# Six start addresses for the transposed input of a hybrid SSD / DeltaNet trunk

## The chip, the cores and the metric

The kernel runs on one core of one Trainium2 chip. The metric is the device time of one execution in microseconds (us); the time before is the median of three runs.

A core has a matrix engine (PE, or TensorE) that multiplies a stationary operand, loaded into its array beforehand, with a moving operand that streams past it; a vector engine (DVE), a scalar engine (ACT), GpSimd (POOL) and SyncE (SP), whose queue issues the transfers here. Operands lie in an on-chip memory of 128 partitions (SBUF); an address below is the byte offset inside a partition. Matrix products are gathered in another on-chip memory (PSUM).

## What is computed

A trunk of two layers on 256 tokens of width 1024. Each layer has three sub-layers, a feed-forward network (FFN), a token mixer, and a second FFN, and each sub-layer starts from a root-mean-square norm of the residual stream:

```python
h = x
for l in range(DEPTH):                                   # DEPTH = 2
    h = h + 0.5 * swiglu(rms_norm(h, ffn1_norm[l]), ffn1_w_in[l], ffn1_w_out[l])
    u = rms_norm(h, mix_norm[l])
    (z_s, xbc, dt_s, qkv, z_d, b_d, a_d, gate_s, gate_d) = split(u @ w_in[l])
    y_s = mamba2_branch(z_s, xbc, dt_s, ...)
    y_d = deltanet_branch(qkv, z_d, b_d, a_d, ...)
    merged = sigmoid(gate_s) * (y_s @ ssm_w_branch[l]) + sigmoid(gate_d) * (y_d @ dn_w_branch[l])
    h = h + merged @ w_out[l]
    h = h + 0.5 * swiglu(rms_norm(h, ffn2_norm[l]), ffn2_w_in[l], ffn2_w_out[l])
return rms_norm(h, final_norm)
```

## The kernel before

**Numbers in two halves.** Every float32 operand of the large products is split into two float32r numbers: a high half, which is the value rounded by ACT, and a low half, the rest, which DVE subtracts. A product a·b is made as three matmuls, high·high, high·low and low·high (`mm3`, `mm3w`).

**The weights.** They stream from device memory in pieces of 128 x 1024 floats. `load` puts a piece into one of five buffers (`wraw`, or `wfirst`), `prep` splits it into `whi` and `wlo`, each with five buffers of 4096 bytes, and `take` hands a piece to the matmuls while it loads and splits the following ones ahead. So a buffer of `whi` or `wlo` comes free when the matmuls have read it.

**The transposed input.** `norm_in`, once for each sub-layer, normalises the residual stream, transposes it on PE (`hnT`) and lets ACT write the high halves and DVE the low halves into `uT` (`rms_chain`). `uT` is one tile of 16384 bytes per partition: for each of the eight blocks of 128 input channels (`kt`) 256 tokens of high halves and then 256 tokens of low halves. It is written once for each of the six sub-layers, and always at the same place.

**Who reads `uT`.** Two kinds of code, which use it in opposite roles:

- `tok_chunk` gives tokens by output channels. The stationary operand is a 128 x 128 slice of `uT`, the moving operand 512 columns of `whi` or `wlo`; lines 287 to 289 (in `mm3`). It makes the tiles `f` (the first chunk of an FFN, 48 matmuls) and `t` (`z` and gate chunks of the mixer, eight units of 48 matmuls in each mixer, so 384).
- `chan_chunk` and `chan_pair` give output channels by tokens. The stationary operand is a 128 x 128 slice of `whi` or `wlo`, the moving operand is `uT`. `chan_pair` (tile `fc`, 20 groups of 16 pairs, so 320 pairs, in each FFN) makes a matmul of 512 columns, the high and the low half of one `kt` together (line 342), and one of 256 columns (line 346). `chan_chunk` (tiles `kk`, `qq`, `vv`, `zd`, `bc`, `xs` of the mixer) makes three matmuls of 256 columns each (lines 292 to 294).

The other large products don't read `uT`: the output products of the FFN (`p`, `o`), the branch products (`b`) and the output product of the mixer (`o` with `mh` and `ml`) have other stationary tiles and moving weights, through `mm3` as well.

**Where things lie.** `uT` starts at byte 32928, which is 160 modulo 256. All buffers of `whi` and `wlo` start at 128 modulo 256 (78464 is the first), and so do `gh`, `gl`, `bsa`, `bsb`, `bsc`, `bh`, `bl`, `mh` and `ml`, the stationary tiles of the other products. All steps inside these tiles that a matmul starts at are multiples of 512 bytes. So every slice of `uT` starts at 160 modulo 256, and every other operand of the large products at 128: the weights lie 224 bytes behind `uT` modulo 256, or, seen from the weights, `uT` lies 32 bytes behind them.

**Order.** The order of work is the program's own, by `FFN` and `ORDER`; a scheduler moves the steps of the norm ahead (`high_priority`). Each engine runs its own list in order.

Of the kernel before, what the change touches and what calls it, by code (L numbers as in the profile page):

```python
# [8 lines left out]
F32R = mybir.dt.float32r  # L9
# [7 lines left out]
P = 128  # L17
D = 1024
S = 256
# [3 lines left out]
KT = D // P  # L23
# [6 lines left out]
NRAW = 5  # L30
NSPL = 5
START = 2

# [16 lines left out]
def trunk_kernel(ctx, tc, x, wst, wsm, norms, lpar, rpar, cst, out):  # L52
# [3 lines left out]
    cpool = ctx.enter_context(tc.tile_pool(name="cpool", bufs=1))  # L56
# [25 lines left out]
    def tmp2(name):  # L82
        return s2.tile([P, 512], F32, tag="s2", name=name)
# [92 lines left out]
    def ahead(key, n, fn):  # L176
        while state[key] < n:
            fn(state[key])
            state[key] += 1
# [47 lines left out]
    Y = [cpool.tile([P, 512], F32, name=f"Y{i}") for i in range(2)]  # L227
    for y in Y:
        G.memset(y[:], 0.0)
    uT = cpool.tile([P, KT, 2, S], F32R, name="uT")  # L230
    uTh, uTl = uT[:, :, 0], uT[:, :, 1]

    def rstd_of(t):

# [9 lines left out]
    def rms_chain(t, nw):  # L244
        r = rstd_of(t)
        hns = []
        for n in range(2):
            hn = tmp2("hn")
            ins = stt(hn[:], h[:, t, n * 512 : (n + 1) * 512], r, nw[n], ALU.mult, ALU.mult)
            hns.append(hn)  # L250
        for n in range(2):
            bank = trb("hnT")
            for k in range(4):
                PE.transpose(bank[:, k * P : (k + 1) * P], hns[n][:, k * P : (k + 1) * P], ident)
            oh = uTh[:, 4 * n : 4 * n + 4, t * P : (t + 1) * P]
            ol = uTl[:, 4 * n : 4 * n + 4, t * P : (t + 1) * P]
            bv = bank[:].rearrange("p (k t) -> p k t", k=4)
            done = [act(oh, bv), tt(ol, bv, f(oh), ALU.subtract)]
        return ins, done

    def norm_in(nw, add=None):

        for t in range(2):
            with tc.high_priority(offset=PRI), ExitStack() as behind:
                if add:
                    add(t)
                    if t == 0:
                        behind.enter_context(tc.issue_after(state["sums"][5].ins))
                ins, done = rms_chain(t, nw)
            if t == 0:  # L270
                state["hold"] = False
                n = state["taken"]
                if not add:
                    ahead("prepped", n + 1, prep)
                    with tc.issue_after(done[0].ins), tc.issue_after(done[1].ins):
                        ahead("prepped", n + START, prep)
                with tc.issue_after(ins.ins):
                    ahead("prepped", n + 2, prep)
                if add:
                    state["behind"][n + 2] = [d.ins for d in done]  # L280
            elif add:

                state["behind"][n + 4] = (state["square"].ins, ins.ins)
                state["input"] = done
# [88 lines left out]
    def residual(po, nw):  # L373
        def add(t):
            for n in range(2):
                hv = h[:, t, n * 512 : (n + 1) * 512]
                stt(hv, po[t][n][:], 0.5, hv, ALU.mult, ALU.add)

        if nw is None:
            return add  # L380
        norm_in(nw, add)
# [154 lines left out]
    def mixer(l, nxt):  # L536
# [686 lines left out]
        close(po, stat, 8, nxt)  # L1223

    norm_in(nw0)
    for l in range(DEPTH):
        ffn(norm_vec(3 * l + 1))
# [3 lines left out]
    for t in range(2):  # L1231
        add(t)
        o = [tmp2("fo") for _ in range(2)]
# [141 lines left out]
```

## Time and profile before

| what | us |
|---|---|
| median of three runs | 1569.11 |
| lowest and highest run | 1568.77 and 1569.37 |
| span of the profiled execution, first to last instruction | 1565.8 |
| PE busy in that span | 1545.0 |
| DVE busy | 1302.4 |
| ACT busy | 999.8 |

The record of the profiled execution gives its span; it lies 3.3 us below the median of the runs, which also hold what comes before the first and after the last instruction.

The profile names an instruction by its line in the kernel, its engine and `out<-in`, the tile that it writes and the tiles that it reads. A matmul's duration in it is modelled and overlaps with that of the next one, so the pace of PE is read from the starts of instructions that follow one another, not from their durations. The chain of waits is followed back from the last instruction, at each step to whatever released it. The six sub-layers begin, by the start of their first `hnT`, at 7.0, 189.4, 600.2, 783.2, 964.9 and 1375.1 us.

### The profile page before, as it was taken

How to read it: one execution, taken by the hardware profiler on the slowest of the kernel's cores; microseconds unless marked ns; L12 is line 12 of the kernel's file. 1: busy time of each engine (PE TensorE's matmuls, PEld its weight loads, DVE VectorE, ACT ScalarE, POOL GpSimd, SP SyncE). 2: the span in 40 equal slices, each digit the busy share in tenths (PEclk: the TensorE clock that was granted, in tenths of full speed). 3: DMA queues.
4: the chain of work that ended last, by engine and by line, in shares of the span. 5: the costliest groups of instructions: out<-in, count | busy, mean ns of one | idle time of the engine just before them, and what ended most of it. 6: DMA issues, size and time to landing. Idle time of an engine off the chain costs nothing.

```text
span 1565.8 us, 26672 instructions
## 1 busy us (share of the span) xinstructions
PE 1545.0 (99%) x10152; PEld 1342.0 (86%) x10152; DVE 1302.4 (83%) x2048; ACT 999.8 (64%) x1694; POOL 53.2 (3%) x60
## 2 busy tenths in 40 slices
PE   8999999999999999999999999999999999999998
PEld 6888779999888888888788887899998888888886
DVE  6889969957899766899878998699579996679897
ACT  6666668766675655666566676686656666466664
POOL 0000010000000000000000001010000000000000
PEclk9999999999999999999999999999999999999999
DMA  8565565553455555465765566555336546555553
GB/s 298 197 214 188 195 212 173 178 158 118 174 207 173 177 205 196 159 210 177 262 204 187 168 198 223 189 189 189 116 123 213 177 166 212 201 175 166 198 189 134
DMA packets 94215, 292.99 MB, mean 187 GB/s; under 512 B 22325, under 2 KB 23301, under 8 KB 93062
## 3 DMA queue, kind: packets, MB, share of 16 engines
q1 hardware_dynamic: 94086, 291.29, 55.2%
q8 instruction: 79, 1.29, 0.3%
q14 instruction: 50, 0.41, 0.1%
HBM read 289.33 MB, written 1.92 MB: 186 GB/s over the span
## 4 chain that ended last, share of the span: by engine, by line
PE 76%; DVE 13%; DMA 5%; issue 3%; ACT 2%; POOL 1%; SPq 0%; POOLq 0%; DVEq 0%; ACTq 0%
PE fc L342 15%; PE fc L346 8%; DVE wlo L69 7%; PE t L287 3%; PE t L288 3%; PE t L289 3%; DMA wraw<-in_wst_dram 3%; PE b L289 3%; PE b L288 3%; PE b L287 2%; PE xs L292 2%; PE xs L293 2%; PE xs L294 2%; PE o L288 1%; PE o L289 1%
## 5 line engine op out<-in xcount | busy, mean ns | idle before, releaser
L69 DVE TENSOR_TENSOR wlo<-wraw,whi 128x1024 fp32r<-128x1024 f32 x488 | 591.0, 1221 | 139.8 <-ACT whi L66 136.1
L66 ACT ACTIVATE whi<-wraw 128x1024 fp32r<-128x1024 f32 x488 | 511.6, 1057 | 176.4 <-PE b L289 29.8
L342 PE MATMUL fc<-uT,whi 128*128 128x512 f32 x1280 | 445.5, 391 | 0.0
L346 PE MATMUL fc<-uT,wlo 128*128 128x256 f32 x1280 | 360.9, 282 | 0.0
L342 PEld LDWEIGHTS fc<-uT,whi 128*128 128x128 f32 x1280 | 240.3, 188 | 50.7
L346 PEld LDWEIGHTS fc<-uT,wlo 128*128 128x128 f32 x1280 | 241.8, 189 | 0.8
L287 PE MATMUL t<-whi,uT 128*128 128x512 f32 x256 | 102.9, 403 | 0.0
L288 PE MATMUL t<-wlo,uT 128*128 128x512 f32 x256 | 101.5, 396 | 0.2 <-DVE wlo L69 0.2
L289 PE MATMUL t<-whi,uT 128*128 128x512 f32 x256 | 101.5, 397 | 0.0
L66 ACT ACTIVATE whi<-wfirst 128x1024 fp32r<-128x1024 f32 x64 | 67.8, 1059 | 29.7 <-DVE wfirst L69 20.4
L66 ACT ACTIVATE sg<-fc 128x256 f32<-128x256 f32 x80 | 30.6, 382 | 82.3 <-PE fc L346 82.3
L69 DVE TENSOR_TENSOR wlo<-wfirst,whi 128x1024 fp32r<-128x1024 f32 x64 | 78.1, 1220 | 2.0 <-ACT whi L66 1.9
L287 PE MATMUL b<-whi,bh 128*128 128x512 f32 x192 | 76.1, 398 | 0.0
L288 PE MATMUL b<-wlo,bh 128*128 128x512 f32 x192 | 74.9, 390 | 0.0
L289 PE MATMUL b<-whi,bl 128*128 128x512 f32 x192 | 74.3, 394 | 0.3 <-DVE bl L69 0.3
L292 PE MATMUL xs<-uT,whi 128*128 128x256 f32 x256 | 73.1, 286 | 0.0
L294 PE MATMUL xs<-uT,wlo 128*128 128x256 f32 x256 | 71.6, 280 | 0.0
L293 PE MATMUL xs<-uT,whi 128*128 128x256 f32 x256 | 71.4, 279 | 0.0
L288 PE MATMUL o<-wlo,gh 128*128 128x512 f32 x160 | 64.6, 404 | 2.6 <-DVE wlo L69 2.5
L69 DVE TENSOR_TENSOR wfirst<-wraw,wfirst 128x1024 f32<-128x1024 f32 x48 | 58.6, 1220 | 8.9 <-DMA wraw<-in_wst_dram 8.9
L289 PE MATMUL o<-whi,gl 128*128 128x512 f32 x160 | 62.5, 391 | 0.0
L287 PE MATMUL o<-whi,gh 128*128 128x512 f32 x160 | 62.1, 392 | 0.0
(317 smaller groups left out, 3424.5 us busy)
## 6 DMA issues: line engine op xcount, KB each, us to landing
wraw<-in_wst_dram SPq DMA_DIRECT2D x504, 512.0 KB, 4.5
wfirst<-in_wst_dram SPq DMA_DIRECT2D x16, 512.0 KB, 5.8
dc<-rdram SPq DMA_DIRECT2D x8, 1024.0 KB, 8.4
nw<-in_norms_dram SPq DMA_DIRECT2D x6, 512.0 KB, 6.2
gb<-rdram SPq DMA_DIRECT2D x8, 256.0 KB, 5.3
h<-in_x_dram SPq DMA_DIRECT2D x4, 256.0 KB, 5.7
out_dram<-fo SPq DMA_DIRECT2D x4, 256.0 KB, 2.1
dq<-X SPq DMA_DIRECT2D x2, 256.0 KB, 5.0
```

Source lines behind the costliest of these rows:

```text
L66: return A.activation(out=o, in_=i, func=func, **kw)
L69: return V.tensor_tensor(out=o, in0=a, in1=b, op=op)
L287: PE.matmul(ps, lh, rh, start=start, stop=False)
L288: PE.matmul(ps, lh, rl, start=False, stop=False)
L289: return PE.matmul(ps, ll, rh, start=False, stop=stop)
L292: PE.matmul(ps, wh, mh, start=start, stop=False)
L293: PE.matmul(ps, wh, ml, start=False, stop=False)
L294: PE.matmul(ps, wl, mh, start=False, stop=stop)
L342: PE.matmul(ps[a][:], wh[:, c0 : c0 + P], uT[:, kt].rearrange("p o t -> p (o t)"), start=kt == 0, stop=False,)
L346: PE.matmul(ps[a][:, 0:S], wl[:, c0 : c0 + P], uTh[:, kt, :], start=False, stop=kt == KT - 1)
```

## The change

`uT` becomes a view into a tile `uW` that is 256 bytes longer, and each sub-layer's `norm_in` takes the view at its own offset. Nothing else is edited.

```diff
 START = 2
+PLACES = [56, 56, 8, 48, 40, 40]
...
-    uT = cpool.tile([P, KT, 2, S], F32R, name="uT")
-    uTh, uTl = uT[:, :, 0], uT[:, :, 1]
+    uW = cpool.tile([P, KT * 2 * S + 64], F32R, name="uW")
+    uT = uTh = uTl = None
+    places = list(PLACES)
+
+    def place_input():
+        nonlocal uT, uTh, uTl
+        o = places.pop(0)
+        uT = uW[:, o : o + KT * 2 * S].rearrange("p (k o t) -> p k o t", k=KT, o=2)
+        uTh, uTl = uT[:, :, 0], uT[:, :, 1]
...
     def norm_in(nw, add=None):
 
+        place_input()
         for t in range(2):
```

The offsets count floats. `uW` starts where `uT` did, at byte 32928, so the six starts and the distances are these:

| sub-layer | offset in bytes | start of `uT` modulo 256 | weights behind `uT`, modulo 256 | `uT` behind the weights, modulo 256 |
|---|---|---|---|---|
| before, all six | 0 | 160 | 224 | 32 |
| 1: FFN 1 of layer 0 | 224 | 128 | 0 | 0 |
| 2: mixer of layer 0 | 224 | 128 | 0 | 0 |
| 3: FFN 2 of layer 0 | 32 | 192 | 192 | 64 |
| 4: FFN 1 of layer 1 | 192 | 96 | 32 | 224 |
| 5: mixer of layer 1 | 160 | 64 | 64 | 192 |
| 6: FFN 2 of layer 1 | 160 | 64 | 64 | 192 |

Everything that is allocated after `uT` moves up by 256 bytes, the weight buffers too, and keeps its remainder modulo 256. The two compiled programs have the same 15534 instructions in the same order on each engine, with the same waits; only start addresses differ.

## The prediction

> **What bounds the kernel now.** I read the page's first and second parts, then who PE waited for, then the chain of waits, then the matmuls grouped by line and tile, and last PE's timeline inside runs of equal matmuls.
>
> ```profile
> span 1565.8 us, 26672 instructions
> PE 1545.0 (99%) x10152; PEld 1342.0 (86%) x10152; DVE 1302.4 (83%) x2048; ACT 999.8 (64%) x1694; POOL 53.2 (3%) x60
> PEclk9999999999999999999999999999999999999999
> ```
>
> ```profile
> PE hnT L254 <- DVE hn L72: 5.1, 7, 1.0
> PE o L288 <- DVE wlo L69: 2.5, 11, 0.8
> PE nw L225 <- DMA row<-in_norms_dram: 2.3, 1, 2.3
> ```
>
> PE has work 99% of the time at an undisturbed clock, and its longest waits in total are 5.1, 2.5 and 2.3 us. So what sets the time is how fast PE starts one matmul after another, and an address can only matter there. The program's order and waits are untouched, so no new wait can come from the edit itself. The chain of waits says where PE's pace counts:
>
> ```profile
> by line: PE fc L342 15.5%; PE fc L346 8.2%; DVE wlo L69 6.9%; PE t L287 3.4%; PE t L288 3.4%; PE t L289 3.4%; DMA wraw<-in_wst_dram 2.9%; issue 2.7%; PE b L289 2.6%; PE b L288 2.5%; PE b L287 2.5%; PE xs L292 1.6%; PE xs L293 1.6%; PE xs L2
> ```
>
> The counts come from the groups by line, tile and shape:
>
> ```profile
> L342 PE MATMUL fc<-uT,whi 128*128 128x512 f32 x1280 | 445.5, 391 | 0.0
> L346 PE MATMUL fc<-uT,wlo 128*128 128x256 f32 x1280 | 360.9, 282 | 0.0
> L287 PE MATMUL t<-whi,uT 128*128 128x512 f32 x256 | 102.9, 403 | 0.0
> L289 PE MATMUL t<-whi,uT 128*128 128x512 f32 x256 | 101.5, 397 | 0.0
> L288 PE MATMUL t<-wlo,uT 128*128 128x512 f32 x256 | 101.5, 396 | 0.2 <-DVE wlo L69 0.2
> L292 PE MATMUL xs<-uT,whi 128*128 128x256 f32 x256 | 73.1, 286 | 0.0
> L292 PE MATMUL bc<-uT,whi 128*128 128x256 f32 x128 | 36.7, 287 | 0.0
> L292 PE MATMUL zd<-uT,whi 128*128 128x256 f32 x128 | 36.3, 284 | 0.0
> L292 PE MATMUL vv<-uT,whi 128*128 128x256 f32 x128 | 36.0, 281 | 0.0
> L292 PE MATMUL qq<-uT,whi 128*128 128x256 f32 x128 | 36.0, 281 | 0.0
> L292 PE MATMUL kk<-uT,whi 128*128 128x256 f32 x128 | 35.9, 281 | 0.0
> L287 PE MATMUL f<-whi,uT 128*128 128x512 f32 x64 | 26.4, 415 | 0.5 <-ACT uT L66 0.5
> ```
>
> Each of these lines runs once per product of halves, three to a product for all but `fc`, and over two mixers or four FFNs. So one mixer has 3 x 256 / 2 = 384 `t` matmuls and 3 x (256 + 5 x 128) / 2 = 1344 of 256 columns with moving `uT`; one FFN has 1280 / 4 = 320 `fc` pairs and 3 x 64 / 4 = 48 `f` matmuls.
>
> Now the pace. These are the first and last rows of undisturbed runs in PE's timeline (start, duration): `t` in the first mixer, `f` in the third FFN, `o` of the first mixer, `b` of the same, then `fc` and `zd`.
>
> ```profile
> 414.35 0.39 PE L288 MATMUL t<-wlo,uT 128*128 128x512 f32 x1
> ...
> 423.68 0.39 PE L289 MATMUL t<-whi,uT 128*128 128x512 f32 x1
> ```
>
> ```profile
> 793.15 0.39 PE L288 MATMUL f<-wlo,uT 128*128 128x512 f32 x1
> ...
> 799.68 0.40 PE L289 MATMUL f<-whi,uT 128*128 128x512 f32 x1
> ```
>
> ```profile
> 584.52 0.39 PE L287 MATMUL o<-whi,mh 128*128 128x512 f32 x1
> ...
> 599.95 0.39 PE L289 MATMUL o<-whi,ml 128*128 128x512 f32 x1
> ```
>
> ```profile
> 567.85 0.39 PE L288 MATMUL b<-wlo,bh 128*128 128x512 f32 x1
> ...
> 577.39 0.39 PE L288 MATMUL b<-wlo,bh 128*128 128x512 f32 x1
> ```
>
> ```profile
> 30.63 0.28 PE L346 MATMUL fc<-uT,wlo 128*128 128x256 f32 x1
> ...
> 69.11 0.28 PE L346 MATMUL fc<-uT,wlo 128*128 128x256 f32 x1
> ```
>
> ```profile
> 319.76 0.28 PE L292 MATMUL zd<-uT,whi 128*128 128x256 f32 x1
> ...
> 325.25 0.28 PE L294 MATMUL zd<-uT,wlo 128*128 128x256 f32 x1
> ```
>
> `t`: 40 steps in 9.33 us, 233.2 ns each. `f`: 28 steps in 6.53 us, 233.2 ns. `o`: 68 steps in 15.43 us, 226.9 ns. `b`: 42 steps in 9.54 us, 227.1 ns. All four go through the same three lines with 512 moving columns of `whi` and `wlo`. What sets `t` and `f` apart is the stationary tile: `uT` at 160 modulo 256, against `mh`, `ml`, `bh`, `bl` at 128 like the weights. So a stationary operand 32 bytes behind the moving one costs 6.3 ns a matmul. `fc`: 111 pairs in 38.48 us, 346.7 ns a pair. `zd`: 47 steps in 5.49 us, 116.8 ns.
>
> **The change part by part.** It removes no instruction and adds none. It moves the start of `uT`, and with it the pace of the matmuls that read `uT`; the rest keeps its distances.
>
> *How much of a saving counts.* By the chain, `t` is on it for 3 x 3.4% of 1565.8 = 159.7 us, of 768 x 233.2 ns = 179.1 us in all: 0.89. `fc` is on it for 23.7%, 371.1 us, of 1280 x 346.7 ns = 443.8 us: 0.84. The rest lies where a split or a transfer sets the pace (`wlo` 6.9%, `wraw` 2.9%); there a faster PE only waits for the next `wlo`. I take 0.89 for `t` and `f`, 0.84 for `fc`, and their middle, 0.87, for the 256-column matmuls.
>
> *`t` in the first mixer.* `uT` then starts at 128 like the weights, exactly the relation of `o` and `b`: 384 x 6.3 ns = 2.42 us, times 0.89, 2.15 us. This is the surest term.
>
> *`t` in the second mixer.* `uT` starts at 64, a distance that no row shows. Bounds: again 2.15 us if any start at a multiple of 64 is as good as 128; a loss of 2.15 us if this distance costs twice what 32 bytes cost. I take +2.15: it is a multiple of 64 as the fast rows are, and the slow row is not.
>
> *`f`.* Three of the four FFNs get a multiple of 64: 48 x 6.3 ns x 0.89 = 0.27 us each, 0.81 together (from -0.81). The FFN at 96 keeps an odd multiple of 32: nothing.
>
> *`fc`.* Here `uT` moves and the weights are stationary. If a pair cost what its parts cost elsewhere, 226.9 + 116.8 = 343.7 ns, it would save 3.0 ns, 320 x 3.0 x 0.84 = 0.81 us an FFN, 2.42 for three. But no row shows an aligned alternation of the two shapes, and the 3.0 ns may be its own cost. I take half, 1.21 us. The ends are far apart: below, 6.3 ns on both matmuls of a pair, -3.4 us an FFN; above, a 256-column matmul at half the aligned 512 step, 113.5 ns, so 6.3 ns a pair saved, +1.7 us an FFN. In the FFN at 96 I take 0.
>
> *The 1344 matmuls of 256 columns in each mixer.* Their step now is 116.8 ns with `uT` at 160, and no row shows another start. Below: 6.3 ns more, 1344 x 6.3 x 0.87 = -7.4 us a mixer. Above: 113.5 ns, 1344 x 3.3 x 0.87 = +3.9 us a mixer. I take nothing, the row itself.
>
> *The writes into `uT`.* Two of ACT and two of DVE for each half of the tokens; on the path they look like this:
>
> ```profile
> 191.59 1.28 DVE uT L69 x2
> ```
>
> If a start changed them by the share by which it changes a `t` matmul, 6.3 of 227, that is 0.04 us here, 0.2 us over six sub-layers. I take nothing.
>
> Sum: 2.15 + 2.15 + 0.81 + 1.21 = 6.3 us. From the profiled span, 1565.8 - 6.3 = 1559.5; the median of the runs lies 3.3 us above the span, so 1562.8 us, 0.4% less.
>
> The Trainium skill speaks against all of this: the page "TensorE: Matmul & The Clock Gate", section "Step-by-step: what each phase is for", gives the matrix engine two independent read ports, one for the moving and one for the stationary operand, and the page "SBUF — State Buffer", section "Specifications (TRN2)", gives lines of 16 bytes, on which every start here falls. By these no start would matter and the sum would be 0. The trace disagrees: 233.2 against 226.9 ns. Whether something other than the address makes `uT` slow is left to the fourth rival.
>
> **The rivals.**
>
> *Only equal starts are fast.* Then sub-layers 1 and 2 gain, 2.15 + 0.27 + 0.40 = 2.8 us, and the other four find other distances as good or bad as now: 1566.3 us. For it: the only fast rows have both operands at 128. Against it: nothing shows that 64 or 192 bytes are as bad as 32.
>
> *Moving reads are slow now as well.* The start at 160 would then cost every 256-column matmul and both of each `fc` pair about 3.3 ns. Half of the 512 step is 113.5, and 116.8 is 3.3 above it; a pair, 346.7, is 6.3 above 226.9 + 113.5. That both gaps come out at about 3.3 ns a matmul speaks for it; that a matmul should have no fixed cost at all speaks against it. It gives `t` and `f` as forecast, 4.3 + 0.8, and 2 x 3.9 from the mixers and 3 x 1.7 from the FFNs: 18.0 us, so 1551.1.
>
> *Slower: 64 bytes behind is a bad distance for a moving `uT`.* In sub-layers 5 and 6 the stationary weights lie 64 bytes behind, in 1344 + 640 matmuls. If each lost what the `t` row loses, 6.3 ns, that is 1984 x 6.3 x 0.84 = 10.5 us, and `t` there gains nothing. Sub-layers 1 to 3 still gain 2.15 + 2 x 0.27 + 2 x 0.40 = 3.5: 7.0 us slower, 1576.1. It turns the sign from 3.5 / (1984 x 0.84) = 2.1 ns a matmul on. For it: a distance of 32 bytes does cost that much in the other role, and where one distance is bad a second may be. Against it: with `uT` moving, the weights 224 bytes behind cost a pair at most 6.3 ns, and no row has a start at a multiple of 64 that is slow.
>
> *Nothing happens.* `t` and `f` are slow for another reason, such as `uT` being just written, or 12 matmuls in a row into one bank. 1569.1 us. Against it: `f` and `t` read `uT` long after it was written, at one constant pace.
>
> **How the numbers follow.** I give the forecast 0.42, only equal starts 0.17, moving reads too 0.20, slower 0.15, nothing 0.06. About 0.2% of 1569 us, 3.1 us, is what a measurement of this kernel can tell from no change. Faster: the forecast nearly whole, 0.39, moving reads 0.20, and a third of the equal starts, 0.06: 0.65. Slower: most of its rival, 0.13, and some mishap of the forecast's unknown distances, 0.03: 0.16. Within the bound: the rest, 0.19. Alone, the forecast's range is 1560 to 1566. To hold 8 in 10 it must reach down to the moving reads, 1551, and up past no change, to 1570; that leaves out the slower case and part of the fast one.
>
> **What would show it.** In the timeline after: `t` steps of 227 ns in both mixers; if they are 227 in the first and 233 in the second, only equal starts are fast. `f` steps of 227 in FFNs 1, 2 and 4 and 233 in the third. `fc` pairs between 344 and 346.7 ns in FFNs 1, 2 and 4 and 346.7 in the third; pairs near 340, with `zd` steps near 113.5, say that moving reads were slow. `zd` or `xs` steps above 119 ns in the second mixer say the slower rival. PE's waits for `wlo` should grow by about 1 us in all and no wait be new. The prediction is wrong if the first mixer's `t` stays at 233, or if a moving operand's distance counts more than a stationary one's.

## The result and the profile after

The change makes the kernel a little slower: 1573.36 us, median of eight runs (1570.54 to 1574.37), against 1569.01 us for eight runs of the kernel before. The ratio is 1.0024, with a 95% interval from 1.0013 to 1.0035. The forecast was 1562.8 us, in a range up to 1570.

The first rows of the page of after, and PE's longest waits in it (total us, times, longest):

```profile
span 1572.0 us, 26672 instructions
PE 1548.3 (98%) x10152; PEld 1341.9 (85%) x10152; DVE 1302.9 (83%) x2048; ACT 1001.3 (64%) x1694; POOL 52.3 (3%) x60
PEclk9999999999999999999999999999999999999999
```

```profile
PE hnT L262 <- DVE hn L73: 6.3, 7, 1.1
PE nw L226 <- DMA row<-in_norms_dram: 2.4, 1, 2.4
PE o L297 <- DVE wlo L70: 2.3, 10, 0.8
```

The clock is whole and the waits are those of before, within about 1 us: no new wait explains 4 us. The time is in PE's pace. A distance from here on is the number of bytes that the weights lie behind `uT`, modulo 256, whichever of the two moves. These are first and last rows of runs in PE's timeline of after, as they were read before: `t` in the first mixer, `zd` in the first mixer, `fc` in the first FFN, all at distance 0; then `t` in the second mixer, and `qq` and `zd` in the second mixer, at distance 64.

```profile
419.31 0.39 PE L297 MATMUL t<-wlo,uW 128*128 128x512 f32 x1
...
428.42 0.39 PE L298 MATMUL t<-whi,uW 128*128 128x512 f32 x1
```

```profile
323.55 0.28 PE L301 MATMUL zd<-uW,whi 128*128 128x256 f32 x1
...
329.19 0.28 PE L303 MATMUL zd<-uW,wlo 128*128 128x256 f32 x1
```

```profile
31.24 0.28 PE L355 MATMUL fc<-uW,wlo 128*128 128x256 f32 x1
...
70.46 0.28 PE L355 MATMUL fc<-uW,wlo 128*128 128x256 f32 x1
```

```profile
1193.58 0.39 PE L297 MATMUL t<-wlo,uW 128*128 128x512 f32 x1
...
1202.76 0.39 PE L298 MATMUL t<-whi,uW 128*128 128x512 f32 x1
```

```profile
1026.12 0.28 PE L301 MATMUL qq<-uW,whi 128*128 128x256 f32 x1
...
1099.59 0.28 PE L301 MATMUL zd<-uW,whi 128*128 128x256 f32 x1
...
1105.12 0.28 PE L303 MATMUL zd<-uW,wlo 128*128 128x256 f32 x1
```

`t` at distance 0: 40 steps in 9.11 us, 227.8 ns, from 233.2: that part came as forecast. `zd` at distance 0: 47 steps in 5.64 us, 120.0 ns, from 116.8. `fc` at distance 0: 111 pairs in 39.22 us, 353.3 ns a pair, from 346.7. At distance 64, `t` takes 229.5 ns and `zd`, 47 steps in 5.53 us, 117.7 ns, while `kk` and `qq` at the start of the same mixer run at 113.3 ns (their rows stand one by one in the timeline; `qq` from 1026.12 to 1031.45 us, 47 steps).

All steps together, sub-layer by sub-layer. A span goes from the start of a sub-layer's first `hnT` to that of the next, the last one to the end. A step is the mean time from the start of a matmul to the start of the next one in the same tile, without gaps over 300 ns; "256" are the mixer's matmuls with moving `uT`, and an `fc` step is half a pair.

| sub-layer | distance after | span before, after | `f` or `t` before, after, ns | `fc` or 256 before, after, ns | steps alone, us |
|---|---|---|---|---|---|
| 1 FFN | 0 | 182.4, 184.8 | 234.6, 229.1 | 173.9, 177.0 | +1.7 |
| 2 mixer | 0 | 410.7, 412.8 | 233.1, 227.9 | 118.4, 121.4 | +2.0 |
| 3 FFN | 192 | 183.0, 184.0 | 233.2, 233.3 | 173.9, 175.7 | +1.1 |
| 4 FFN | 32 | 181.7, 182.4 | 233.1, 233.2 | 173.9, 175.1 | +0.8 |
| 5 mixer | 64 | 410.2, 408.1 | 233.1, 229.4 | 118.4, 116.7 | -3.7 |
| 6 FFN | 64 | 190.7, 192.7 | 232.9, 228.8 | 173.9, 177.1 | +1.8 |

The last column multiplies the changes by their numbers, 48 `f` and 640 `fc` steps in an FFN, 384 `t` and 1344 of 256 columns in a mixer; for sub-layer 2, 1344 x 3.0 ns - 384 x 5.2 ns = +2.0 us. The sum, +3.7 us, agrees with the 0.24% of the result. The spans add up to about 6 us more, but they are of one execution each, and the eight runs of the kernel before already lie up to 4.2 us apart. So every FFN loses where `uT` moves, the first mixer loses there twice what it gains in `t`, and only the second mixer gains.

### The profile page after: what moved, and what is told of

It reads as the page before. It is cut to its first block, busy times and chain, and to the rows that moved or that the text cites. A ratio compares the mean times of both kernels' runs of the same rounds, so it can differ in the third digit from the quotient of the medians.

```text
span 1572.0 us, 26672 instructions
## 1 busy us (share of the span) xinstructions
PE 1548.3 (98%) x10152; PEld 1341.9 (85%) x10152; DVE 1302.9 (83%) x2048; ACT 1001.3 (64%) x1694; POOL 52.3 (3%) x60
## 4 chain that ended last, share of the span: by engine, by line
PE 74%; DVE 13%; DMA 6%; issue 3%; ACT 2%; POOL 1%; SPq 0%; POOLq 0%; DVEq 0%; ACTq 0%
PE fc L351 16%; PE fc L355 8%; DVE wlo L70 6%; DMA wraw<-in_wst_dram 4%; PE t L297 3%; PE t L296 3%; PE t L298 3%; PE b L298 3%; PE b L297 3%; PE b L296 3%; PE p L296 1%; PE p L298 1%; PE p L297 1%; PE xs L303 1%; PE xs L302 1%
## 5 line engine op out<-in xcount | busy, mean ns | idle before, releaser
L351 PE MATMUL fc<-uW,whi 128*128 128x512 f32 x1280 | 451.4, 396 | 0.0
L355 PE MATMUL fc<-uW,wlo 128*128 128x256 f32 x1280 | 359.4, 281 | 0.0
L351 PEld LDWEIGHTS fc<-uW,whi 128*128 128x128 f32 x1280 | 240.5, 188 | 57.6
L355 PEld LDWEIGHTS fc<-uW,wlo 128*128 128x128 f32 x1280 | 240.7, 188 | 0.8
L296 PE MATMUL t<-whi,uW 128*128 128x512 f32 x256 | 101.9, 399 | 0.0
L297 PE MATMUL t<-wlo,uW 128*128 128x512 f32 x256 | 100.5, 393 | 1.0 <-DVE wlo L70 1.0
L298 PE MATMUL t<-whi,uW 128*128 128x512 f32 x256 | 100.5, 392 | 0.0
L301 PE MATMUL xs<-uW,whi 128*128 128x256 f32 x256 | 73.4, 287 | 0.0
L303 PE MATMUL xs<-uW,wlo 128*128 128x256 f32 x256 | 71.9, 281 | 0.0
L302 PE MATMUL xs<-uW,whi 128*128 128x256 f32 x256 | 71.8, 280 | 0.0
```

The source lines that it names most:

```text
L296: PE.matmul(ps, lh, rh, start=start, stop=False)
L297: PE.matmul(ps, lh, rl, start=False, stop=False)
L298: return PE.matmul(ps, ll, rh, start=False, stop=stop)
L301: PE.matmul(ps, wh, mh, start=start, stop=False)
L302: PE.matmul(ps, wh, ml, start=False, stop=False)
L303: PE.matmul(ps, wl, mh, start=False, stop=stop)
```

## The experiments

The theory after the result: the pace of a matmul follows the distance between the starts of its two operands modulo 256, in both roles of `uT`, and the distance that is best for one role is not the best for the other. The rivals: it follows the start of `uT` itself; or it comes from the 256 bytes by which the other tiles moved. The diffs are against the kernel after the change.

**The longer tile alone.**

```diff
-PLACES = [56, 56, 8, 48, 40, 40]
+PLACES = [0, 0, 0, 0, 0, 0]
```

> The longer tile alone: uT stays at 160 modulo 256 in all six sub-layers, everything behind it moves up by 256 bytes. Distance theory (the pace of a matmul follows the distance between the starts of its two operands modulo 256) and start theory (it follows the start of uT itself): as before, 1569 us, t 233.2 ns, 256-column matmuls 116.7 ns, fc pairs 346.7 to 347.8 ns. Shift theory (it is the 256 bytes by which the other tiles moved): about 1573 us, as after.

1569.25 us, ratio to before 1.0001 (0.9991 to 1.0010). `t` steps 233.2, `fc` steps 173.9, 256 columns 118.4 ns, as before. The shift of the other tiles costs nothing that shows, within 0.1%, and 256 bytes more of distance change no pace.

**The weights moved in place of the input.**

```diff
-PLACES = [56, 56, 8, 48, 40, 40]
+PLACES = [0, 0, 0, 0, 0, 0]
...
-    uW = cpool.tile([P, KT * 2 * S + 64], F32R, name="uW")
+    uW = cpool.tile([P, KT * 2 * S + 8], F32R, name="uW")
```

> uT stays at 160 modulo 256, and everything behind it, the weights too, moves up by 32 bytes, also to 160: the distance is 0 in all six sub-layers at the old start of uT. Distance theory: the paces of sub-layers 1 and 2 after the change everywhere, t 227 ns, 256-column matmuls 120.0 ns, fc pairs 353 to 354 ns, and mixers 2 us and FFNs 2 us longer than before, so about 1581 us. Start theory: as before, t 233, 256-column 116.7, fc 347, 1569 us.

1577.99 us, ratio 1.0053 (1.0039 to 1.0067). The same three runs of its timeline, `t` and `zd` in the first mixer and `fc` in the first FFN:

```profile
416.25 0.40 PE L297 MATMUL t<-wlo,uW 128*128 128x512 f32 x1
...
425.36 0.39 PE L298 MATMUL t<-whi,uW 128*128 128x512 f32 x1
```

```profile
321.40 0.28 PE L301 MATMUL zd<-uW,whi 128*128 128x256 f32 x1
...
327.04 0.28 PE L303 MATMUL zd<-uW,wlo 128*128 128x256 f32 x1
```

```profile
30.87 0.28 PE L355 MATMUL fc<-uW,wlo 128*128 128x256 f32 x1
...
70.09 0.28 PE L355 MATMUL fc<-uW,wlo 128*128 128x256 f32 x1
```

`uT` has not moved, and the steps are those of after at distance 0: 9.11 us for 40 `t`, 5.64 us for 47 `zd`, 39.22 us for 111 `fc` pairs, each the same to 0.01 us. Start theory is out: with another start for both operands and the same distance the pace is the same. This was done for distance 0 alone; every other distance below was made by moving `uT`. The forecast of 1581 us was 3 us too high: the steps alone grew by about 11 us, the time by 8, so not all of the loss arrived.

**The two halves of the change.** The FFNs alone, then the mixers alone, each with the other sub-layers at the old start:

```diff
-PLACES = [56, 56, 8, 48, 40, 40]
+PLACES = [56, 0, 8, 48, 0, 40]
```

> The FFNs as after the change, both mixers at the old start. Distance theory, with the paces read in the profile of after: fc steps longer by 3.1, 1.7, 1.2 and 3.2 ns in sub-layers 1, 3, 4 and 6, 640 of them each, 5.9 us; f 6 ns shorter in 48 matmuls of sub-layer 1 and 4 ns in 48 of sub-layer 6, 0.5 us; so 5.4 us slower than before, about 1575 us. The prediction's own terms: 2 us faster.

```diff
-PLACES = [56, 56, 8, 48, 40, 40]
+PLACES = [0, 56, 0, 0, 40, 0]
```

> The mixers as after the change, the FFNs at the old start. Distance theory: the first mixer +4.0 us in 1344 matmuls of 256 columns and -2.0 us in 384 t; the second -2.3 and -1.4 us; 1.7 us faster in all, about 1567.5 us, and with the run before this one the whole change, 3.7 us slower. The prediction's own terms: 4.3 us faster.

The FFNs alone: 1573.66 us, ratio 1.0033 (1.0021 to 1.0045), 5.2 us slower where the steps say 5.4. The mixers alone: 1568.88 us, ratio 0.9994 (0.9983 to 1.0006), so 0.9 us faster with an interval that holds both the 1.7 us of the steps and no change. Together -0.06% and +0.33% make 0.27%, the change's 0.24% within the intervals. So the loss is the FFNs', as far as these intervals tell.

**Both mixers at 64.**

```diff
-PLACES = [56, 56, 8, 48, 40, 40]
+PLACES = [0, 40, 0, 0, 40, 0]
```

> The FFNs at the old start (distance 224), both mixers at the start that sub-layer 5 has after the change (distance 64). Distance theory: FFNs as before, fc pairs 347; both mixers 2.1 us shorter than before, as sub-layer 5 was (408.1 against 410.2 us), so about 1565 us. If the 2.1 us of sub-layer 5 were a chance of that one execution: 1569 us.

1563.74 us, ratio 0.9962 (0.9949 to 0.9975): 6 us faster than before, nearly what the steps give, 2 x 3.7 us, and more than the 4 us of the expectation, which had gone by one span. The 256-column steps are 116.6 ns and `t` 229.4 and 229.6 in both mixers; `fc` stays at 173.9.

**All other distances.** Four kernels give each sub-layer a distance of its own; only their profiles count here.

```diff
-PLACES = [56, 56, 8, 48, 40, 40]
+PLACES = [16, 24, 24, 32, 32, 4]
```

> Distances not yet seen, read by sub-layer in the profile: weights behind uT by 160, 128, 128, 96, 96 and 208 bytes modulo 256 in sub-layers 1 to 6. Distance theory with few modes: fc pairs between 340 and 355 ns, 256-column matmuls at 113.3, 116.7, 117.8 or 120.0 ns (steps of 272, 280, 283 or 288 cycles), t between 227 and 233. Start theory: the starts at multiples of 64 (sub-layers 2 and 3 at 0 modulo 256) alike, and unlike those at odd multiples of 32 and of 16. No forecast of the time, 1560 to 1580 us.

```diff
+PLACES = [52, 8, 44, 36, 48, 28]
```

> More distances, read by sub-layer: weights behind uT by 16, 192, 48, 80, 32 and 112 bytes modulo 256 in sub-layers 1 to 6. Distance theory: in each sub-layer one steady pace, or two that alternate by what ran before; fc pairs between 340 and 355 ns, 256-column matmuls between 113 and 121 ns; the mixer at 32 shows for its moving uT what FFN 1 of layer 1 showed after the change. A rival, that only steps of 32 bytes matter: 16 like 0 (354 ns a pair), 48 like 32 or 64, 80 like 64 or 96, 112 like 96 or 128.

```diff
+PLACES = [60, 16, 12, 20, 36, 39]
```

> The remaining distances: weights behind uT by 240, 160, 176, 144, 80 and 68 bytes in sub-layers 1 to 6. Distance theory as in the run before. If a mixer comes below the 406.8 us of a mixer at 64, or an FFN below the 181.1 us of one at 224, that distance is the better one for it.

```diff
+PLACES = [55, 39, 63, 38, 41, 37]
```

> Distances that are no multiple of 16: weights behind uT by 4, 68, 228, 72, 60 and 76 bytes in sub-layers 1 to 6. If single bytes of distance count, as the 345.4 ns of an fc pair at 68 against 354 at 64 says, the paces differ from those at 0, 64 and 224; FFNs at 72 and 76 then lie near 346 ns a pair; a mixer at 60 or 68 may lie below the 406.8 us of one at 64. If only blocks of 16 or 32 bytes count: 4 like 0 (354 ns), 68 like 64, 228 like 224 (346.7 to 347.8).

The four ran in 1574.95, 1577.3, 1580.55 and 1577.9 us, one run each. The mean steps in ns, with those of before and after, by distance:

| distance | `fc` | 256 columns | `t` |
|---|---|---|---|
| 0 | 177.0 | 121.4 | 227.9 |
| 4, 16 | 176.9, 176.9 | | |
| 32 | 175.1 | 119.9 | 233.2 |
| 48 | 176.5 | | |
| 60 | | 123.1 | 233.3 |
| 64 | 177.1 | 116.7 | 229.4 |
| 68 | 172.7 | 120.0 | 233.1 |
| 72, 76 | 176.0, 179.2 | | |
| 80 | 175.4 | 120.8 | 230.1 |
| 96 | 173.9 | 119.7 | 233.4 |
| 112 | 173.8 | | |
| 128 | 175.9 | 120.3 | 232.5 |
| 144 | 177.0 | | |
| 160 | 175.5 | 121.5 | 234.2 |
| 176 | 177.0 | | |
| 192 | 175.7 | 118.7 | 233.3 |
| 208, 240 | 173.8, 173.9 | | |
| 224 (before) | 173.9 | 118.4 | 233.1 |
| 228 | 172.1 | | |

Most values are of one sub-layer in one execution, and a mean can mix more than one pace. At 192, `fc` has 175.7 ns here and 174.9 in the same FFN of the run with the FFNs alone: of stretches of eight pairs, 12 of 33 ran at 353 to 354 ns a pair after the change and none there, where all ran at 349 to 350. So differences of under 1 ns in this table are not shown to come from the distance.

The expectation of a few modes held for the size, not for its list: the steps lie anywhere between 172.1 and 179.2 for `fc`. That 72 and 76 would be fast like 68 was wrong, and so was every rule by multiples of 16, 32 or 64: 60, 64 and 68 give 123.1, 116.7 and 120.0 ns. And what is good for `fc` (68) is bad for the 256-column matmuls, and the other way round (64).

**A break in front of the matmuls.** In both mixers at distance 64, the 256-column matmuls ran at two steady paces at the same distance. From the timeline of that kernel's first mixer, `qq` in the run of chunks that starts behind the small float32 products `psp` and `lb`, and `zd` in the run that starts behind a chunk with stationary `uT`:

```profile
245.33 0.28 PE L301 MATMUL qq<-uW,whi 128*128 128x256 f32 x1
...
250.66 0.28 PE L303 MATMUL qq<-uW,wlo 128*128 128x256 f32 x1
...
318.80 0.28 PE L301 MATMUL zd<-uW,whi 128*128 128x256 f32 x1
...
324.33 0.28 PE L303 MATMUL zd<-uW,wlo 128*128 128x256 f32 x1
```

47 steps each, 5.33 and 5.53 us: 113.4 and 117.7 ns. To see whether the place in the program sets that, one float32 matmul, or four (`range(4)`), was put between, on top of the kernel with both mixers at 64; what it writes is overwritten:

```diff
     def tok_chunk(ps, ks):
...
+        state["tok"] = True
     def chan_chunk(ps):
         ws = [take(), take()]
+        if state.pop("tok", False):
+            for _ in range(1):
+                PE.matmul(ps[:, 0:P], ident, ident, start=True, stop=True)
```

> Mixers at 64, FFNs at 224, and one float32 matmul of 128 x 128 x 128 put in front of each chunk of 256-column matmuls that follows a chunk with stationary uT; its result is overwritten. Theory that the pace is a locked phase between the two read streams that the preceding work sets: the 256-column matmuls behind a t unit, at 117.8 ns in both mixers so far, change to another of the steady paces, most likely 113.3 ns, and keep it to the next break. Rival, that the pace belongs to the place in the program (the buffers, the accumulator, the load of the other engines): still 117.8 ns.

> The same with four float32 matmuls instead of one, so that no 512-column matmul is near. Locked phase: 113.3 ns behind every t unit, or at least not 117.8 everywhere. Rival: 117.8 ns.

With one, the same `zd`, and the break in front of the `vv` before it:

```profile
306.78 0.38 PE L328 MATMUL vv<-cs 128*128 128x128 f32 x2
...
317.91 0.28 PE L301 MATMUL zd<-uW,whi 128*128 128x256 f32 x1
...
323.24 0.28 PE L303 MATMUL zd<-uW,wlo 128*128 128x256 f32 x1
```

Now 47 steps take 5.33 us, 113.4 ns: the pace changed at the break and lasted through `vv`, `zd` and the `bc` that follows. At the break before that one, at 295 us, the pace stayed at 117.8 ns, so a break may change the pace and need not; with four matmuls it was 113.3 ns behind both, though not behind every break: the `xs` matmuls behind the fourth ran at 113.4 ns in the first mixer and at 117.8 in the second. The addresses of these `vv` and `zd` matmuls are the same with and without a break. So addresses alone don't set the pace: a matmul put in just before can change it, and the pace then lasts. It bought nothing: the mixers took 406.9 and 408.1 us with one break, against 406.8 and 408.9, and 413.3 and 414.3 with four, whose 20 matmuls a mixer take 4.1 us themselves (1562.15 and 1576.02 us, one run each).

Nor do the addresses and the order of the work together set it. The kernel with both mixers at 64 and the one of the next experiment have the same mixers, with the same operand addresses in the same order. These are the second and the last row of one run of `bc` in the first mixer, in the former kernel and then in the latter:

```profile
365.27 0.28 PE L302 MATMUL bc<-uW,whi 128*128 128x256 f32 x1
...
370.50 0.28 PE L303 MATMUL bc<-uW,wlo 128*128 128x256 f32 x1
```

```profile
363.57 0.28 PE L302 MATMUL bc<-uW,whi 128*128 128x256 f32 x1
...
368.99 0.28 PE L303 MATMUL bc<-uW,wlo 128*128 128x256 f32 x1
```

46 steps each, 5.23 and 5.42 us: 113.7 and 117.8 ns. Something else decides here, perhaps the exact times of the work before; what it is isn't shown.

**The best distances seen, together.**

```diff
-PLACES = [56, 56, 8, 48, 40, 40]
+PLACES = [63, 40, 63, 63, 40, 63]
```

> The best distances seen: FFNs at 228, mixers at 64. Distance theory: fc steps of 172.1 ns in all four FFNs as in sub-layer 3 of the run before, 1.8 ns below those at 224, 4 x 640 of them, 4.6 us; the mixers as with 64 alone, 6 us (ratio 0.9962); together about 10 us faster than before, a ratio near 0.993. If the pace at 228 was only the chance of one sub-layer, some FFNs stay near 174 ns and the ratio is 0.9962.

1562.47 us, ratio to before 0.9950 (0.9937 to 0.9964): 8 us faster than the kernel before, not the 10 that were expected, and not clearly faster than with the mixers alone (0.9962). The pace came in all four FFNs, 172.1 ns. In the first, 111 pairs now take 38.11 us, where before they took 38.48:

```profile
31.10 0.28 PE L355 MATMUL fc<-uW,wlo 128*128 128x256 f32 x1
...
69.21 0.28 PE L355 MATMUL fc<-uW,wlo 128*128 128x256 f32 x1
```

But the FFNs didn't get shorter: 181.7, 182.6, 181.8 and 192.1 us, against 183.8, 181.4, 181.1 and 191.2 with the mixers alone. PE's wait for `wlo` in the output products, in the kernel with the mixers alone and then in this one:

```profile
PE o L297 <- DVE wlo L70: 1.5, 9, 0.2
```

```profile
PE o L297 <- DVE wlo L70: 4.3, 15, 0.8
```

2.8 us more than there, and 1.7 to 2.2 more than in the other profiled kernels with all FFNs at 224 (2.1 to 2.6 us). Those kernels, six with the one above, show where the gain went. From the first to the last `fc`, the four FFNs together took 532.7 us in each of the six and 528.5 here; from the last `fc` to the next sub-layer they took 135.4 to 138.8 us in the six and 141.8 here. There DVE and the weight transfers set the pace, and a PE that comes earlier waits. A loss in the FFNs alone reached the end whole (5.2 of 5.4 us). Of the 4.6 us gained in the steps the two ratios show 1.9 us, about 3 us either way, and the spans of the one execution show none.

## Why the prediction was wrong

The forecast gained 6.3 us and the steps lost 3.7, so 10.0 us have to be explained. Term by term, the forecast with its factors for the path and the steps without: `t` in the first mixer +2.15 and +2.0 us, `t` in the second +2.15 and +1.4, `f` +0.81 and +0.5, `fc` +1.21 and -5.9, the 256-column matmuls 0 and -1.7. The step that failed is the pace of the matmuls with moving `uT`, `fc` above all: 7.1 of the 10.0 us. It met the prediction's own sign of being wrong, that a moving operand's distance counts more than a stationary one's: -7.6 against +3.9 us.

*What bounds the kernel* was right: PE's pace, and no new wait.

*That distance matters* was right: the run with the weights moved shows 120.0 against 116.8 ns and 227.8 against 233.2 ns by distance alone. The Trainium skill's page "TensorE: Matmul & The Clock Gate", section "Step-by-step: what each phase is for", gives the matrix engine two independent read ports. By that rule alone no start would matter, and these runs disagree.

*`t` in the first mixer*, the surest term, was right: 5.2 ns for each of 384, 2.0 us, against 2.15. With `f` in the first FFN it was also the only term with a row of the very same distance in the same role.

*`t` in the second mixer and `f` in three FFNs* went by "a multiple of 64 is good". 64 gave 3.7 ns in `t`, where 0 gave 5.2; 192 gave nothing in `f`, and 128 and 192 next to nothing in `t`. The rule was drawn from one fast start and one slow one.

*The 1344 matmuls of 256 columns* are where the forecast put a term at nothing: "I take nothing, the row itself". That row, 116.8 ns, was one pace at one distance and said nothing of others. They lost 3.0 ns in the first mixer, 4.0 us, and won 1.7 ns in the second, 2.3 us, both inside the bounds of -7.4 and +3.9 us a mixer.

*`fc`* failed most, and in sign: half of 3.0 ns a pair was booked as a gain, 1.21 us, and 0 for the FFN at 32; the four FFNs lost 6.2, 3.5, 2.4 and 6.3 ns a pair, 5.9 us in all. The reference for the gain, 226.9 ns in `o` at distance 0, was a matmul of equal shapes in a row; in the alternation of 512 and 256 columns, at that same distance, a pair takes 353.3 ns and not 343.7. The forecast carried a pace from one role and one pattern to another.

*How much of a saving counts*, 0.84 to 0.89 for gains and losses alike, is left open: of the FFNs' loss 5.2 of 5.4 us arrived, of the mixers' gain at 64 some 6 of 7.4, and of the 4.6 us gained in the FFNs in the last experiment 1.9, about 3 us either way, which holds both 0.84 and nothing.

*The rivals.* "Slower" had the kind of mechanism right, a bad distance for a moving `uT`, and the wrong place: 64 was good for the 256-column matmuls and bad for `fc`, and distance 0, which it counted as a gain, was bad for both. "Moving reads are slow now as well" fell: 224 is among the better distances for a moving `uT`. "Only equal starts are fast" came nearest for `t`, where distance 0 was the fastest, but 64 and 80 gained 3.7 and 3.0 ns there, where 0 gained 5.2, and it had nothing to say of the losses.

*The range* ended at 1570 because cases with a loss in the moving role were given 0.15. The bounds had it, 7.4 us in a mixer and 3.4 us in each FFN, and the moving role is that of 2 x 1344 + 4 x 640 = 5248 of the 6208 matmuls that the change touches, `t` and `f` being the other 960; the bounds were named and then not used.

## What to carry to other kernels

Where PE is the bound, the distance between the starts of a matmul's two operands is worth a sweep: here several per cent of a step (172.1 to 179.2 ns in `fc`), and 0.4% of the kernel by moving one tile. It has to be measured for each pattern of shapes and each role by itself, in one profile with a distance for each stage; a good distance doesn't carry from one to another. A faster stage counts only if what follows it isn't waiting for something else.

## What was not expected of the hardware

Steps of four bytes count: the 256-column matmuls take 123.1, 116.7 and 120.0 ns at 60, 64 and 68 bytes, and an `fc` step 172.7 at 68 and 179.2 at 76. And one pair of addresses has more than one steady pace, 113.3 and 117.8 ns, kept for some two hundred matmuls in a row. A matmul put in before can change it, and the same work at the same addresses took either pace in two executions. Both fit two streams of reads that get in each other's way by their phase, but no trace shows such reads; that cause is argued, not shown.
